# GpSimd's copies of the input into the second token order: from one block of sixteen to two blocks of eight, between and behind the rotations

## The chip, the cores and the metric

The kernel runs on one core of a Trainium2 chip. The metric is the device time of one execution in microseconds. The engines of the core are TensorE (PE; its weight loads are listed as PEld), VectorE (DVE), ScalarE (ACT), GpSimd (POOL) and SyncE (SP), which issues most DMAs. Each engine works through its own instructions in order and waits for others by semaphores.

## The reference

The reference is a decoder trunk of two layers on 512 tokens of 1024 channels, all in float32. Only the attention of the first layer matters here:

```python
qkv = xn @ w_qkv
q, k, v = jnp.split(qkv, 3, axis=-1)
q = apply_rope(q.reshape(B, T, A_HEADS, HEAD_DIM), cos, sin)
k = apply_rope(k.reshape(B, T, A_HEADS, HEAD_DIM), cos, sin)
...
for g, (window, r) in enumerate(A_GROUPS):
    ...
    o, lse = banded_attention(gather(q), gather(k), gather(v), window // r)
```

There are three groups of four heads, with (window, dilation) = (128, 1), (512, 4) and (2048, 16). With dilation r the tokens are taken in the order "every r-th token first": `gather` sorts the tokens by their place modulo r. The rotation (`apply_rope`) changes 16 of the 64 channels of every head of the queries and keys. Behind the attention come a gated convolutional feed-forward part, a second layer with full attention, and another feed-forward part.

## The kernel before, in words

Every large product is made of three float32r products: the operands are split into a high and a low part, and `mm3` (lines 228 to 231) adds high × high, high × low and low × high in PSUM. So the normed input of the first layer, transposed to channels × tokens, exists as four tiles: high and low part, each for channels 0 to 511 (index 0) and 512 to 1023 (index 1). They are called `xT` (line 549; xah and xal in the profile). Each is 128 partitions × 4 channel groups × 512 tokens.

Group 0 of the heads works on the tokens in their own order. Groups 1 and 2 work on a second order, in which the tokens are sorted by their place modulo 4. For these the kernel keeps the same four tiles once more with the tokens in that order, `xP` (line 550; xph and xpl). GpSimd makes them: `reorder(b)` (lines 556 to 562) copies the 128 tokens of block b, one instruction of 128 × 512 elements for each of the four tiles. Since each block of the second order has a quarter of its tokens from every block of the first, no part of `xP` can be used for a product before all four blocks are copied.

The order of the work in the first stage is written out by hand (lines 751 to 824), and each engine's instructions come in the order of these lines:

- Lines 751 to 781: for each token block, the norm, the transposes into `xT` (`transpose0`) and the query and key products of group 0 (`qk0`). `qk_post` (lines 569 to 582) follows for each block: ScalarE copies the product out of PSUM (line 573), then GpSimd rotates it with four instructions (lines 579 to 582). The four calls of `reorder` stand behind the rotations of blocks 0 and 1 and ahead of those of blocks 2 and 3.
- `v_proj0` (lines 708 to 724): the value products of group 0. Between them stand `qk_transpose(0, b)` (lines 584 to 591), in which TensorE transposes the rotated queries and keys and VectorE copies them out of PSUM (line 591), and `scores(0, 0)` and `scores(0, 1)`: TensorE's products of queries and keys (line 613), the softmax's first pass on VectorE (line 598) and the exponential on ScalarE (line 599).
- `wide_proj(1, ...)` (lines 783 to 797): the query and key products of group 1, on `xP`. It goes through the four weight tiles one by one, and for each through the four blocks. The first two weight tiles meet channels 0 to 511, the last two channels 512 to 1023. Between the weight tiles stand `p_transpose` (TensorE at line 635, ScalarE's copies at lines 637 and 640) and further scores of group 0.
- `wide_proj(2, ...)` and `wide_proj(1, "v_ps", ...)` follow for group 2 and for the values of both groups, and then the rest of the attention.

Weights come through the class `Weights` (lines 27 to 67): SyncE loads a tile, ScalarE writes its high part (line 49) and VectorE its low part (line 55), some tiles ahead of their use. The tiles of 8 KB per partition (weights, `xT`, `xP`, the queries and keys, the transposed probabilities) come from one pool of 17 buffers, so that new tiles take the place of old ones as soon as their last reader is done.

Of the kernel before, what the change touches and what calls it, by code (L numbers as in the profile page):

```python
# [8 lines left out]
F32 = mybir.dt.float32  # L9
# [7 lines left out]
NB = 4  # L17
# [53 lines left out]
def trunk_kernel(ctx, tc, x, norm_gains, w_qkv_a, w_o_a, w_q_b, w_o_b, kv_norm, w_kvf, b_f,  # L71
                 w_up, conv_w, conv_b, w_down, rope, out):
    nc = tc.nc
    act, dve, pool, pe, sp = nc.scalar, nc.vector, nc.gpsimd, nc.tensor, nc.sync
# [8 lines left out]
    def t8(shape, dt=F32, name="t8"):  # L83
        return p8.tile(shape, dt, tag="t8", name=name)
# [4 lines left out]
    def t2(shape, dt=F32, name="t2"):  # L89
        return p2.tile(shape, dt, tag="t2", name=name)  # L90

    def bank(shape, name="bank"):
        return psp.tile(shape, F32, tag="ps", name=name)
# [134 lines left out]
    def mm3(o, ah, al, bh, bl, first, last, shared=False):  # L228
        pe.matmul(o, ah, bh, start=first, stop=False, skip_group_check=shared)  # L229
        pe.matmul(o, ah, bl, start=False, stop=False, skip_group_check=shared)  # L230
        pe.matmul(o, al, bh, start=False, stop=last, skip_group_check=shared)  # L231
# [55 lines left out]
    def new_xT(name):  # L287
        hi = [t8([128, 4, T], F32R, name=f"{name}h{i}") for i in range(2)]
        lo = [t8([128, 4, T], F32R, name=f"{name}l{i}") for i in range(2)]
        return hi, lo  # L290
# [258 lines left out]
    xT = new_xT("xa")  # L549
    xP = new_xT("xp")  # L550
    xn = {}

    def by_fourth(a, spec="p k (l r) -> p k r l"):
        return a.rearrange(spec, r=4)

    def reorder(b):

        for part in range(2):
            for i in range(2):
                src = by_fourth(xT[part][i][:, :, b * 128:b * 128 + 128])  # L560
                dst = xP[part][i].rearrange("p k (r l) -> p k r l", r=4)[:, :, :, b * 32:b * 32 + 32]
                pool.tensor_copy(dst, src.bitcast(F32))

    def ax(g, b, kc):
        return xs(xP if g else xT, kc, slice(b * 128, b * 128 + 128))
# [3 lines left out]
    def qk_post(g, b, o):  # L569
        if b == 0:  # L570
            qks[g] = t8([128, 4, 8, HD], name=f"qk{g}")
        qk = qks[g][:, b]
        act.copy(qk.rearrange("p a d -> p (a d)"), o)
        tu = t2([128, 2, 8, 16], name="tu")
        rb = 4 * min(g, 1) + b
        c2 = rp[:, rb, None, 0:16].to_broadcast([128, 8, 16])
        s_lo = rp[:, rb, None, 16:24].to_broadcast([128, 8, 8])
        s_hi = rp[:, rb, None, 24:32].to_broadcast([128, 8, 8])
        pool.tensor_tensor(tu[:, 0], qk[:, :, 0:16], c2, ALU.mult)
        pool.tensor_tensor(tu[:, 1, :, 0:8], qk[:, :, 8:16], s_lo, ALU.mult)  # L580
        pool.tensor_tensor(tu[:, 1, :, 8:16], qk[:, :, 0:8], s_hi, ALU.mult)
        pool.tensor_tensor(qk[:, :, 0:16], tu[:, 0], tu[:, 1], ALU.add)
# [153 lines left out]
    def transpose0(b):  # L736
        transpose_in(b, xn.pop(b), xT)

    def qk0(b, *pieces):
        if b not in qk_banks:  # L740
            qk_banks[b] = bank([128, T], name="qk_ps")
        for s in pieces:
            if s not in ws:
                ws[s] = [t.rearrange("p (k c) -> p k c", k=2) for t in W.get()]
            wh, wl = ws[s]
            for k in range(2):
                kc = 2 * s + k
                ah, al = ax(0, b, kc)
                mm3(qk_banks[b], ah, al, wh[:, k, :], wl[:, k, :], kc == 0, kc == KD - 1)
# [18 lines left out]
    qk0(1, 3)  # L768
    qk_post(0, 0, qk_banks[0])
    qk_post(0, 1, qk_banks[1])  # L770
    qk0(2, 0, 1)
    transpose0(3)
    for b in range(NB):
        reorder(b)
    qk0(2, 2, 3)
    W.split(5)
    qk_post(0, 2, qk_banks[2])
# [1 line left out]
    W.ahead = 4  # L779
    W.split(6)  # L780
    qk_post(0, 3, qk_banks[3])

    def wide_proj(g, name, post, between):

        banks = [bank([128, T], name=name) for _ in range(4)]
        for s in range(4):
            w = W.get()
            wh, wl = (t.rearrange("p (k c) -> p k c", k=2) for t in w)
            for b in range(4):
                for k in range(2):  # L790
                    kc = 2 * s + k
                    ah, al = ax(g, b, kc)
                    mm3(banks[b], ah, al, wh[:, k, :], wl[:, k, :], kc == 0, kc == KD - 1)
                if s == 3:
                    post(g, b, banks[b])
            for f in between[s]:
                f()
# [348 lines left out]
    for n in range(N + 3):  # L1146
        live = n < N
        if live:
            j, i = units[n]
# [81 lines left out]
```

## Time and profile before

| | |
|---|---|
| median of 3 runs | 1174.08 us (1173.22 to 1174.54) |
| the profiled execution | 1175.93 us |
| its span in the profile | 1174.1 us |
| mean granted TensorE clock | 0.996 |
| GpSimd busy in 0 to 30, 30 to 60, 60 to 75 us | 7.21, 22.07, 0.00 us |
| VectorE busy in 30 to 60 us | 14.16 us |
| TensorE busy in 0 to 30, 30 to 60, 60 to 75 us | 27.64, 27.18, 14.84 us |

The profile is one execution, and its times count from the start of its span. A row of the timeline gives the start, the length, the engine, the line, the operation, the tiles it writes and reads, and how many instructions are merged in it; in brackets stands how long the engine was idle before it and what ended that. Matmuls overlap each other, so how long a row of them holds TensorE is read from the start of one row to the start of the next. The granted clock is the share of full speed that TensorE's clock was given.

### The profile page before, as it was taken

The page shows a single profiled execution, that of the slowest core. Times are in us where ns is not written, and L with a number is a line of the kernel's source. Part 1 is how long each engine was busy: PE and PEld are TensorE (multiplying, and loading weights), DVE is VectorE, ACT ScalarE, POOL GpSimd, SP SyncE. Part 2 cuts the span into 40 slices and gives each one's busy share as a digit, 9 for nine tenths or more (in the row PEclk, how much of TensorE's full clock was granted, in tenths as well). Part 3 has the DMA queues.
Part 4 walks back from the last instruction along what each step waited for, and adds up shares of the span by engine and source line. Part 5 has one row for each costly group of instructions (what it writes and reads, how often), then busy time and mean ns, then how long its engine had stood idle before and what let it go on. Part 6 is the DMA issues. An engine that isn't in the chain of part 4 may idle for free.

```text
span 1174.1 us, 15132 instructions
## 1 busy us (share of the span) xinstructions
PE 1157.1 (99%) x5898; PEld 962.0 (82%) x5898; DVE 666.9 (57%) x991; ACT 517.1 (44%) x900; POOL 204.2 (17%) x231
## 2 busy tenths in 40 slices
PE   9999999999999999999999999999999999999997
PEld 6788889888888888888778888789888888888886
DVE  6433477565566575406465688847565565575304
ACT  5354565433334354305462577755343333354202
POOL 2722000122122120000000466500122122120000
PEclk9899999999999999999999999999999999999999
DMA  8121064332333345302304343364333332344001
GB/s 292 54 91 55 1 166 126 90 105 79 103 108 88 92 137 189 88 1 58 107 1 127 90 118 117 91 201 126 90 92 88 108 105 78 105 132 173 1 1 71
DMA packets 134849, 115.72 MB, mean 99 GB/s; under 512 B 5753, under 2 KB 119913, under 8 KB 134778
## 3 DMA queue, kind: packets, MB, share of 16 engines
q1 hardware_dynamic: 133498, 110.57, 31.1%
q0 software_dynamic: 1280, 4.20, 1.5%
q8 instruction: 46, 0.75, 0.3%
q14 instruction: 25, 0.20, 0.1%
HBM read 108.41 MB, written 2.15 MB: 94 GB/s over the span
## 4 chain that ended last, share of the span: by engine, by line
PE 86%; DVE 5%; ACT 4%; POOL 2%; issue 2%; DVEq 0%; ACTq 0%
PE up L229 12%; PE up L230 12%; PE up L231 12%; PE acc L229 9%; PE acc L231 9%; PE acc L230 9%; PE v_ps L229 2%; PE v_ps L231 2%; PE v_ps L230 2%; PE qk_ps L229 1%; PE qk_ps L230 1%; PE qk_ps L231 1%; PE first L231 1%; PE first L229 1%; PE first L230 1%
## 5 line engine op out<-in xcount | busy, mean ns | idle before, releaser
L55 DVE TENSOR_TENSOR w<-wraw,w 128x1024 fp32r<-128x1024 f32 x182 | 264.6, 1480 | 94.3 <-ACT w L49 93.9
L49 ACT CAST w<-wraw 128x1024 fp32r<-128x1024 f32 x182 | 185.5, 1051 | 61.4 <-PE acc L231 38.2
L517 ACT ACTIVATE bb<-up,conv 128x512 f32<-128x512 f32 x80 | 62.6, 782 | 272.4 <-PE up L231 272.4
L525 POOL TENSOR_TENSOR hT<-bb 128x512 f32<-128x512 f32 x44 | 92.8, 2110 | 490.8 <-DVE bb L520 348.8
L518 DVE SCALAR_TENSOR_TENSOR bb<-up,conv,bb 128x511 f32<-128x511 f32 x80 | 60.0, 749 | 172.9 <-ACT bb L517 172.9
L229 PE MATMUL acc<-w,hs 128*128 128x512 f32 (+1 forms) x356 | 137.9, 387 | 1.1 <-DVE mix L276 1.1
L230 PE MATMUL acc<-w,hs 128*128 128x512 f32 (+1 forms) x356 | 137.6, 387 | 0.0
L231 PE MATMUL acc<-w,hs 128*128 128x512 f32 (+1 forms) x356 | 137.6, 387 | 0.0
L229 PE MATMUL up<-xbh,w 128*128 128x512 f32 x320 | 124.5, 389 | 0.0
L229 PE MATMUL up<-xch,w 128*128 128x512 f32 x320 | 124.5, 389 | 0.0
L230 PE MATMUL up<-xbl,w 128*128 128x512 f32 x320 | 124.5, 389 | 0.0
L230 PE MATMUL up<-xcl,w 128*128 128x512 f32 x320 | 124.5, 389 | 0.0
L231 PE MATMUL up<-xbh,w 128*128 128x512 f32 x320 | 124.5, 389 | 0.0
L231 PE MATMUL up<-xch,w 128*128 128x512 f32 x320 | 124.5, 389 | 0.0
L229 PEld LDWEIGHTS acc<-w,hs 128*128 128x128 f32 x356 | 66.8, 188 | 14.8 <-DVE mix L276 1.3
L230 PEld LDWEIGHTS acc<-w,hs 128*128 128x128 f32 x356 | 66.8, 188 | 13.7
L231 PEld LDWEIGHTS acc<-w,hs 128*128 128x128 f32 x356 | 66.8, 188 | 13.5
L231 PEld LDWEIGHTS up<-xbh,w 128*128 128x128 f32 x320 | 60.1, 188 | 12.6
L231 PEld LDWEIGHTS up<-xch,w 128*128 128x128 f32 x320 | 60.1, 188 | 12.6
L229 PEld LDWEIGHTS up<-xbh,w 128*128 128x128 f32 x320 | 60.1, 188 | 12.5
L230 PEld LDWEIGHTS up<-xcl,w 128*128 128x128 f32 x320 | 60.1, 188 | 12.5
L229 PEld LDWEIGHTS up<-xch,w 128*128 128x128 f32 x320 | 60.1, 188 | 12.3
(241 smaller groups left out, 2092.3 us busy)
## 6 DMA issues: line engine op xcount, KB each, us to landing
wraw<-in_w_up_dram SPq DMA_DIRECT2D x88, 512.0 KB
wraw<-in_w_down_dram SPq DMA_DIRECT2D x44, 512.0 KB
wraw<-in_w_kvf_dram SPq DMA_DIRECT2D x16, 512.0 KB
wraw<-in_w_qkv_a_dram SPq DMA_DIRECT2D x16, 256.0 KB
wraw<-in_w_q_b_dram SPq DMA_DIRECT2D x8, 512.0 KB
ck<-cd SPq DMA_DIRECT2D x8, 512.0 KB
qst<-qst POOLq DMA_DIRECT2D x16, 256.0 KB, 3.4
wraw<-in_w_o_b_dram SPq DMA_DIRECT2D x8, 512.0 KB
```

The lines of the kernel that those rows point to most:

```text
L49: self.nc.scalar.copy(pair[:, 0], raw)
L55: self.nc.vector.tensor_tensor(pair[:, 1], raw, pair[:, 0].bitcast(F32), ALU.subtract)
L229: pe.matmul(o, ah, bh, start=first, stop=False, skip_group_check=shared)
L230: pe.matmul(o, ah, bl, start=False, stop=False, skip_group_check=shared)
L231: pe.matmul(o, al, bh, start=False, stop=last, skip_group_check=shared)
L517: act.activation(bb[:, s, :], ps, AF.Identity, bias=cp[:, 3, ch:ch + 1], scale=cp[:, 2, ch:ch + 1])
L518: dve.scalar_tensor_tensor(bb[:, s, 1:], ps[:, :T - 1], cp[:, 1, ch:ch + 1], bb[:, s, 1:], ALU.mult, ALU.add)
L525: pool.tensor_tensor(hT[c // 4][:, c % 4, :], bb[:, 0, :], bb[:, 1, :], ALU.mult)
```

## The change

`reorder` takes several blocks, and within a call goes through the channel halves first, then the blocks, then the high and low part. It is called twice: for blocks 0 and 1 behind the rotations of blocks 0 and 1, and for blocks 2 and 3 behind the rotations of blocks 2 and 3. The number of copies, their shapes and their operands stay as they are.

```diff
-    def reorder(b):
-
-        for part in range(2):
-            for i in range(2):
-                src = by_fourth(xT[part][i][:, :, b * 128:b * 128 + 128])
-                dst = xP[part][i].rearrange("p k (r l) -> p k r l", r=4)[:, :, :, b * 32:b * 32 + 32]
-                pool.tensor_copy(dst, src.bitcast(F32))
+    def reorder(*blocks):
+
+        for i in range(2):
+            for b in blocks:
+                for part in range(2):
+                    src = by_fourth(xT[part][i][:, :, b * 128:b * 128 + 128])
+                    dst = xP[part][i].rearrange("p k (r l) -> p k r l", r=4)[:, :, :, b * 32:b * 32 + 32]
+                    pool.tensor_copy(dst, src.bitcast(F32))
...
     qk_post(0, 0, qk_banks[0])
     qk_post(0, 1, qk_banks[1])
+    reorder(0, 1)
     qk0(2, 0, 1)
     transpose0(3)
-    for b in range(NB):
-        reorder(b)
     qk0(2, 2, 3)
     W.split(5)
     qk_post(0, 2, qk_banks[2])
     qk0(3, 0, 1, 2, 3)
     W.ahead = 4
     W.split(6)
     qk_post(0, 3, qk_banks[3])
+    reorder(2, 3)
```

From line 557 on the changed kernel's lines stand one further down, so the copies are line 563 there, the rotations 580 to 583, the transposes 589 and the scores 614.

## The prediction

> **What bounds the kernel now.** I read the page first, then the waits of TensorE, then the first stage by windows, then its timeline.
>
> ```profile
> span 1174.1 us, 15132 instructions
> ## 1 busy us (share of the span) xinstructions
> PE 1157.1 (99%) x5898; PEld 962.0 (82%) x5898; DVE 666.9 (57%) x991; ACT 517.1 (44%) x900; POOL 204.2 (17%) x231
> ```
>
> TensorE is busy for 1157.1 of 1174.1 us, so a change off TensorE counts only where TensorE stands still or runs slow. GpSimd's own 204.2 us are worth nothing by themselves. The waits of TensorE over the whole span (total, times, longest) begin with the place that this change touches:
>
> ```profile
> PE qkT_ps L588 <- POOL qk L582: 2.8, 2, 2.4
> ```
>
> The longest is the transpose of the rotated queries and keys (L588), which waits for GpSimd's rotation (L582). The windows (length, busy time of PE, PEld, DVE, ACT, POOL, then clock, DMA share, GB/s) show that it costs more than those 2.8 us:
>
> ```profile
> 48.40:57.80 9.40, 6.58 (x29) 4.91 (x29) 3.72 (x18) 4.45 (x14) 3.67 (x9) 0.64 0.00 1
> 57.80:100.00 42.20, 42.04 (x221) 34.63 (x220) 14.06 (x43) 18.70 (x51) 7.23 (x16) 1.00 0.26 89
> 100.00:500.00 400.00, 399.84 (x2028) 336.19 (x2027) 235.60 (x296) 177.24 (x281) 55.24 (x40) 1.00 0.34 102
> ```
>
> ```profile
> 53.33:57.77 4.44, 4.44 (x20) 3.53 (x20) 3.00 (x16) 2.55 (x11) 0.00 (x0) 0.50 0.00 0
> 68.61:71.88 3.27, 3.11 (x25) 2.46 (x25) 2.00 (x11) 1.53 (x7) 0.00 (x0) 1.00 0.00 0
> ```
>
> From 53.33 to 57.77 the granted clock is 0.50. A mean of 0.64 over the 9.4 us comes out when it is 0.50 for 9.4 × 0.36 / 0.5 = 6.8 us of them, the last ones: from about 51.0 to 57.8. The stall is followed by 6.8 us at half speed. Its timeline there (start, length):
>
> ```profile
> 48.02 0.28 PE L230 MATMUL v_ps<-w,xah 128*128 128x256 f32 x1
> 48.14 0.28 PE L231 MATMUL v_ps<-w,xal 128*128 128x256 f32 x1
> 50.79 1.05 PE L588 MATMUL qkT_ps<-ident,qk 128*128 128x128 f32 x4 [2.37 <-POOL qk L582]
> 52.28 1.11 PE L588 MATMUL qkT_ps<-ident,qk 128*128 128x128 f32 x4 [0.45 <-POOL qk L582]
> 53.33 3.09 PE L613 MATMUL s_ps<-qkT 64*128 64x128 f32 x16
> 56.35 0.79 PE L229 MATMUL qk_ps<-w,xph 128*128 128x512 f32 x1
> ...
> 57.77 0.39 PE L229 MATMUL qk_ps<-w,xph 128*128 128x512 f32 x1
> ```
>
> Between the last value product (48.14) and the fourth product of the second projection (57.77) stand eight transposes, sixteen score rows and three products. And here is why GpSimd is late:
>
> ```profile
> 27.17 2.19 POOL L562 CAST xph<-xah 128x512 fp32r<-128x512 f32 x2
> ...
> 37.57 3.24 POOL L562 CAST xph<-xah 128x512 fp32r<-128x512 f32 x2
> ...
> 49.19 0.45 POOL L579 TENSOR_TENSOR tu<-qk,rope 128x128 f32<-128x128 f32 x1
> ...
> 51.78 0.45 POOL L582 TENSOR_TENSOR qk<-tu 128x128 f32<-128x128 f32 x1
> ```
>
> Sixteen copies (L562) run without a pause from 27.17 to 49.19. The rotations of token blocks 2 and 3 stand behind them and end at 52.23.
>
> **The change, part by part.** No instruction is added or taken away on any engine; GpSimd's are put in another order. In the instruction order of the changed kernel, eight copies (blocks 0 and 1) follow the rotations of blocks 0 and 1, then come the eight rotation instructions of blocks 2 and 3, then the other eight copies: four of channels 0 to 511 first, then four of the rest. No DMA moves. TensorE gains waits: the first products of wide_proj(1) wait for GpSimd's low copies, those of its third weight for the high ones. In GpSimd's queue the late copies move behind the rotations; behind them stand the rotations of group 1, whose input comes only from products that need the copies anyway.
>
> *Rotations, the part on the path.* The first eight copies now take 27.17 to 37.57 (the eight of before have the same shapes, and ScalarE and VectorE write blocks 0 and 1 earlier still). The rotations take 52.23 − 49.19 = 3.04, so they end at 40.6. Their input of block 3 is there:
>
> ```profile
> 36.09 0.59 ACT L573 COPY qk<-qk_ps 128x512 f32<-128x512 f32 x1 [3.90 <-PE qk_ps L231]
> ```
>
> It ends at 36.7. TensorE asks for the rotations at 48.26, 7.6 us after their end. Both waits at L588, 2.8 us, go.
>
> *What is late next* is the copies in front of wide_proj(1). Copies have two lengths, and so have VectorE's weight splits (L55) beside them (shortest, median, longest, in ns):
>
> ```profile
> L562 POOL CAST xph<-xah x8: 1092/1134/2153, 27.2 to 46.0; 128x512 fp32r<-128x512 f32 x8
> ```
>
> ```profile
> L55 DVE TENSOR_TENSOR w<-wraw,w x4: 1224/2150/2157, 37.7 to 59.9; 128x1024 fp32r<-128x1024 f32 x4
> ```
>
> ```profile
> 37.66 6.30 DVE L55 TENSOR_TENSOR w<-wraw,w 128x1024 fp32r<-128x1024 f32 x3 [4.12 <-ACT w L49]
> 43.89 0.68 DVE L591 COPY qkT<-qkT_ps 128x512 f32<-128x512 f32 x1
> ```
>
> At the short length sixteen copies would take 16 × 1.09 = 17.4; they took 22.0, so some 4.6 us are lost to splits, about 1.05 a split. Three splits (37.66 to 43.96) now meet the rotations and the first late copies. No row shows a rotation beside a split. Its price is between nothing and one whole short split each, 3 × 1.22 = 3.7; I take the copies' 1.05, the nearest row; even at 3.7 the rotations end at 44.3, in time. The low copies then end at 37.57 + 3.04 + 4 × 1.09 + 3 × 1.05 = 48.1 (45.0 without any loss; 52.9 with 3.7 on the rotations and all four copies at 2.15). TensorE wants them at 50.9 (below): 2.8 us of cover, and at the bad end 2.0 us of a new wait. The high copies end at 52.5, at 56.7 if all four are long, at 61.5 from the bad end. They are wanted 15.5 us behind the first wide product (56.35 to 71.88, next fence), at 66.4.
>
> *VectorE beside the late copies.* The copies of 48 to 52 us lie beside VectorE's L591 and its softmax, as none did before. L591 took 0.68 at 43.89 with a copy beside it: no price. The softmax has no such row; I take nothing, and at most the splits' factor, 2.15 / 1.22, on its first 2 us or so: 1.5 us. What hides it: the transposes that need it stand a full weight's products (6.2 us) behind the scores, and scores and exponentials took 3.2 us (53.33 to 56.49):
>
> ```profile
> 56.10 0.39 ACT L599 ACTIVATE p<-p,st 128x128 f32<-128x128 f32 x1
> ```
>
> ```profile
> 62.59 0.60 PE L635 MATMUL pT_ps<-ident,p 128*128 128x128 f32 x4
> ```
>
> ScalarE's L640 and three weight casts (L49) wait for late copies because they reuse the copied tiles' memory; the queue behind them waits too. The earliest, L640, comes after those transposes, 57 us in the new count, later than every copy it needs.
>
> *The sum.* What the stretch takes at full clock, from the same work elsewhere:
>
> ```profile
> 41.64 1.04 PE L588 MATMUL qkT_ps<-ident,qk 128*128 128x128 f32 x8
> 42.44 0.36 PE L229 MATMUL v_ps<-w,xah 128*128 128x256 f32 x1
> ```
>
> ```profile
> 68.61 2.10 PE L613 MATMUL s_ps<-qkT 64*128 64x256 f32 x16
> 70.81 1.31 PE L635 MATMUL pT_ps<-ident,p 128*128 128x128 f32 x8
> 71.88 0.48 PE L229 MATMUL qk_ps<-w,xph 128*128 128x512 f32 x1
> ```
>
> ```profile
> 96.98 1.56 PE L615 MATMUL s_ps<-qkT 64*128 64x128 f32 x16
> 98.47 0.50 PE L229 MATMUL qk_ps<-w,xph 128*128 128x512 f32 x1
> ...
> 99.27 0.40 PE L229 MATMUL qk_ps<-w,xph 128*128 128x512 f32 x1
> ```
>
> Eight transposes: 42.44 − 41.64 = 0.80. Scores: half are 128 wide, half 256; 1.49 for sixteen of one kind, 2.20 of the other, so 1.85 (between 1.51, half of what they took at half clock, and 2.20). Three products: 0.80. The last value product holds TensorE until 48.14 + 0.12 = 48.26. So the first wide product starts at 48.26 + 0.80 + 1.85 = 50.9 and the fourth at 51.7, where it started at 57.77: **6.1 us less**, 5.7 to 6.4 by the bounds of the scores. Of this 2.8 is the stall and 3.3 the half clock. Behind 57.8 TensorE stands busy (42.04 of 42.20 us, then 399.84 of 400) and everything that feeds it is released by its own progress; the DMA share in the stretch is 0.00, so no transfer is being waited out. The gain goes to the end.
>
> The profiled execution took 1175.93 (span 1174.1 and 1.8 around it), 1.85 above the median of 1174.08. 1175.93 − 6.1 = 1169.8 against it, or **1168.0** against the median.
>
> **The rivals.**
>
> *The stall goes, the low clock stays.* If transposes and short scores are too light to keep the clock, the new stretch (2.65 us of them) still halves it for some 6.8 us and loses 3.4: the gain is 2.7, **1171.4**. Against it stands the window 68.61 to 71.88: 3.27 us of scores and transposes at 1.00. For it: the clock fell after only 2.4 us without work. The Trainium skill, "TensorE: Matmul & The Clock Gate", Part 1, has the clock fall after an idle window of about 3.4 us and rise after a busy one. By that rule 2.4 us alone would not do it, the light work around the stall would have to count as idle, and the sum would be this rival's. The trace disagrees on the length but agrees that a fall is paid for over more than one window.
>
> *The wait moves to wide_proj(1), and the kernel is slower.* Place: the first wide product, which waits for the four late low copies. If every copy, early and late, takes the long 2.15, they end at 27.17 + 12 × 2.15 + 3.04 = 56.0. TensorE idles 5.1 us, the clock halves, and 6.8 us at half follow: 56.0 + 0.80 + 3.4 = 60.2 against 57.77, 2.4 us slower, **1176.5**. It breaks even where the copies end at 53.6. For it: copies do double beside splits. Against: only about five of sixteen did, and VectorE has no splits between 43.96 and the softmax. The Trainium skill, "SBUF — State Buffer", "Who interferes with whom", lets a VectorE instruction with two SBUF inputs contend with GpSimd's reads and one with at most one input there not. By it the softmax (one input in PSUM) would lengthen no copy; the 0.68 of L591 agrees for a PSUM copy, and no run here shows it for the softmax.
>
> *Nothing is gained*, because rotations stay late or a later wait takes it back: **1174.1**. The instruction order and the 7.6 us of cover speak against the first, the busy windows against the second.
>
> **How the numbers follow.** The forecast gets 0.82, the low clock 0.06, the moved wait 0.06 (0.04 of it slower), nothing gained 0.06. Faster by over 0.2% (2.35 us, about what a measurement can tell from no change): 0.82 + 0.06 + 0.01 = 0.89. Within: 0.06 + 0.01 = 0.07; slower: 0.04. The forecast's own range is 1167.7 to 1168.4 by the sum, and the three runs of before lie 0.9 below to 0.5 above their median, so 1166.8 to 1168.9. At the bad end of the low copies, a wait of 2.0, the time is 1170.0; I take 1166.8 to 1170.2, which leaves out the three rivals, 0.18.
>
> **What would show it.** Right: no wait at L588, transposes at about 48.3, the first wide product near 50.9, rotations ended by 41 to 44, clock 1.00 throughout 48 to 58, TensorE 1.00 busy there. Wrong: a wait of the first wide product for L563 (the copies' line after), a clock of 0.50 anywhere up to 60, a split or softmax longer than 2.2, or a TensorE wait behind 60 us that is new.

## The result, and the profile after

The changed kernel takes 1169.16 us (median of 6 runs, 1168.86 to 1169.52); the kernel before, run beside it, takes 1173.76 (6 runs, 1172.74 to 1175.50). The ratio is 0.996, with a 95% interval of 0.9947 to 0.9972: faster by 4.6 us, 0.4%. The prediction said 1168.0, with a range of 1166.8 to 1170.2. The profiled execution took 1168.88, with a span of 1167.1, 7.0 us shorter than that of before.

The waits of TensorE over the whole span of the changed kernel no longer have a row of GpSimd; those of the second layer lead:

```profile
PE o_ps L1120 <- ACT pT L1107: 1.5, 1, 1.5
PE v_ps L229 <- ACT xkh L431: 1.4, 1, 1.4
```

The window of the stall (columns as in the prediction: length, busy time of five engines, granted clock, DMA share, GB/s) and the one behind it:

```profile
48.40:57.80 9.40, 9.40 (x57) 7.70 (x56) 4.74 (x19) 7.46 (x24) 3.57 (x4) 1.00 0.00 1
57.80:100.00 42.20, 42.14 (x224) 34.80 (x223) 14.68 (x42) 19.07 (x50) 7.21 (x16) 1.00 0.30 100
```

TensorE is busy for all of the 9.40 us, where it was for 6.58, and the clock is 1.00, where it was 0.64. Its timeline in that place:

```profile
48.05 0.28 PE L231 MATMUL v_ps<-w,xal 128*128 128x256 f32 x1
48.17 1.04 PE L589 MATMUL qkT_ps<-ident,qk 128*128 128x128 f32 x8
49.13 1.68 PE L614 MATMUL s_ps<-qkT 64*128 64x128 f32 x16
50.75 0.50 PE L229 MATMUL qk_ps<-w,xph 128*128 128x512 f32 x1
...
51.55 0.39 PE L229 MATMUL qk_ps<-w,xph 128*128 128x512 f32 x1
```

The eight transposes follow the value products at once, and the fourth wide product starts at 51.55 instead of 57.77: 6.2 us earlier. GpSimd's timeline shows why:

```profile
36.43 1.13 POOL L563 CAST xpl<-xal 128x512 fp32r<-128x512 f32 x1
37.52 0.46 POOL L580 TENSOR_TENSOR tu<-qk,rope 128x128 f32<-128x128 f32 x1
37.95 1.30 POOL L581 TENSOR_TENSOR tu<-qk,rope 128x64 f32<-128x64 f32 x1
39.21 1.31 POOL L582 TENSOR_TENSOR tu<-qk,rope 128x64 f32<-128x64 f32 x1
40.59 1.32 POOL L583 TENSOR_TENSOR qk<-tu 128x128 f32<-128x128 f32 x1
...
42.97 0.46 POOL L583 TENSOR_TENSOR qk<-tu 128x128 f32<-128x128 f32 x1
43.38 1.13 POOL L563 CAST xph<-xah 128x512 fp32r<-128x512 f32 x1
...
46.59 1.14 POOL L563 CAST xpl<-xal 128x512 fp32r<-128x512 f32 x1
...
50.85 1.11 POOL L563 CAST xpl<-xal 128x512 fp32r<-128x512 f32 x1
```

The rotations end at 43.4, 4.7 us before TensorE asks for them; the low copies (channels 0 to 511) end at 47.7, 3.0 us before the first wide product; the high ones (channels 512 to 1023) at 52.0. Three of the rotation's instructions last 1.3 us; they met VectorE's weight splits.

So the mechanism is the one forecast: the rotations come early, the wait goes, and the clock stays up. What didn't fit was the size: between the two profiles the stretch gained 6.2 and the spans 7.0, and the medians only 4.6.

### The profile page after: what moved, and what is told of

Its sections match the earlier page's. It is cut to its first block, busy times and chain, and to the rows that moved or that the text cites. A ratio compares the mean times of both kernels' runs of the same rounds, so it can differ in the third digit from the quotient of the medians.

```text
span 1167.1 us, 15131 instructions
## 1 busy us (share of the span) xinstructions
PE 1153.6 (99%) x5898; PEld 960.1 (82%) x5898; DVE 663.8 (57%) x991; ACT 515.8 (44%) x900; POOL 203.9 (17%) x231
## 4 chain that ended last, share of the span: by engine, by line
PE 89%; DVE 5%; ACT 3%; issue 2%; DVEq 0%; ACTq 0%
PE up L231 12%; PE up L229 12%; PE up L230 12%; PE acc L229 9%; PE acc L230 9%; PE acc L231 9%; PE v_ps L229 2%; PE v_ps L231 2%; PE v_ps L230 2%; PE qk_ps L230 2%; PE qk_ps L229 2%; PE qk_ps L231 2%; PE first L229 1%; PE first L230 1%; PE first L231 1%
## 5 line engine op out<-in xcount | busy, mean ns | idle before, releaser
L517 ACT ACTIVATE bb<-up,conv 128x512 f32<-128x512 f32 x80 | 62.4, 780 | 272.8 <-PE up L231 272.8
L231 PEld LDWEIGHTS up<-xch,w 128*128 128x128 f32 x320 | 60.1, 188 | 12.6
L230 PEld LDWEIGHTS up<-xbl,w 128*128 128x128 f32 x320 | 60.1, 188 | 12.5
```

The source lines that it names most:

```text
L517: act.activation(bb[:, s, :], ps, AF.Identity, bias=cp[:, 3, ch:ch + 1], scale=cp[:, 2, ch:ch + 1])
```

## The experiments

**Theory A**: the half clock behind the stall has no fixed length; the profiled execution of before had a long one, and in the median less of it was saved. **Theory B**, the rival: the half clock is always the same, and 1.5 us of the gain are given back later. Further rivals were about which half of the change does it. The time of the kernel before, run beside the experiments, had a median of 1175.74 in the first four and of 1174.64 in the last four.

**The kernel before again** (no edit).

> The kernel before, unchanged, run again to see how its executions differ from each other. The change gained 4.6 us in the medians (1173.76 to 1169.16), 6.2 in the stretch between the two profiles and 7.0 over their spans. Theory A: the half clock behind the stall isn't of one length; it was 6.8 us in the profiled execution and is shorter in most. Then the executions of this kernel spread by some 3 us, from about 1172.5 to 1176, the fast ones with a mean granted clock near 1.000 and the slow ones near 0.996, and a new profile shows the half clock at another place or length, with the same wait of about 2.4 us at the transposes. Theory B: the half clock is the same in every execution and some 1.5 us of the gain are given back later. Then clock and time hardly vary (0.996, within 1 us) and the profile looks as it did.

Measured: 1175.16 (11 runs, 1172.95 to 1175.92), ratio 0.9996 (0.9987 to 1.0005). With all runs of the unchanged kernel whose clock was listed there are 55 executions, with a median of 1175.01. By their mean granted clock:

| clock | executions | shortest, median, longest (us) |
|---|---|---|
| 0.999 | 8 | 1172.74, 1173.03, 1173.91 |
| 0.998 | 12 | 1174.27, 1174.81, 1175.19 |
| 0.997 | 5 | 1173.91, 1174.14, 1175.02 |
| 0.994 to 0.996 | 30 | 1174.56, 1175.77, 1176.69 |

They spread over 4.0 us, and the short ones have nearly the full clock. The classes overlap because the clock also falls at other places: in the last microseconds, in which TensorE has nothing left to do (0.50 and 0.00 us busy in the last 2 us of the new profile), and in some executions in the second layer (below). Time and clock vary as theory A has it, and not as B has it. The new profile, by windows:

```profile
48.40:57.80 9.40, 6.67 (x31) 4.92 (x30) 3.33 (x15) 4.07 (x13) 4.06 (x10) 0.64 0.00 1
```

Here the fall was as long as in the first profile (mean 0.64), in an execution of 1175.50. This profile by itself would have fitted B too.

**The stall filled.** Products that nothing reads keep TensorE at work while it waits:

```diff
+    def fill(n):
+        o = bank([128, 512], name="fill")
+        for _ in range(n):
+            pe.matmul(o, xT[0][0][:, 0, 0:128], xT[0][0][:, 0, :], start=True, stop=True)
...
-             [L(qk_transpose, 0, 2), L(qk_transpose, 0, 3), ...
+             [L(fill, 10), L(qk_transpose, 0, 2), L(fill, 4), L(qk_transpose, 0, 3), ...
```

> The kernel before, with products that nothing reads put into the stall: ten 128x512 products ahead of the transposes of block 2 and four ahead of those of block 3. TensorE is kept at work while it waits, so the stall stays and the half clock should go. At full clock the waits alone cost what lies between 48.26 (or 48.2) and the end of the last rotation, 52.2, less one block's transposes, 0.4: 3.6 us. Theory A (the clock's share differs from execution to execution, 1 us on average): 1169.2 + 3.7 = 1172.9, with a spread of under 1 us, so 0.9 below the kernel before. Theory B (the clock always costs 2.5 us beyond the wait): the same 3.7 above the changed kernel if nothing is given back, but 2.5 below the kernel before: 1171.3. Rival: the clock has nothing to do with idleness; then the profile still shows 0.50 behind 51 us and the time is that of before, 1173.8.

Measured: 1173.04 (11 runs, 1172.69 to 1173.63), ratio to before 0.9983 (0.9974 to 0.9992). The window and the timeline of TensorE:

```profile
48.40:57.80 9.40, 9.34 (x53) 7.10 (x52) 3.73 (x18) 5.68 (x19) 3.71 (x9) 1.00 0.00 1
```

```profile
48.31 2.46 PE L809 MATMUL fill<-xah 128*128 128x512 f32 x10
50.82 0.66 PE L588 MATMUL qkT_ps<-ident,qk 128*128 128x128 f32 x4
51.23 1.17 PE L809 MATMUL fill<-xah 128*128 128x512 f32 x4
52.33 0.66 PE L588 MATMUL qkT_ps<-ident,qk 128*128 128x128 f32 x4
...
55.32 0.39 PE L229 MATMUL qk_ps<-w,xph 128*128 128x512 f32 x1
```

Useless work made the kernel faster: the transposes are as late as before (50.82 and 52.33), but the clock stays at 1.00 and the fourth wide product comes at 55.32. The spread shrinks to 0.9 us. What is left above the changed kernel, 1173.04 − 1169.16 = 3.9, is the price of the wait alone, against 3.7 expected. The rest of what the kernel before loses is mostly the clock's, and it varies. Against the kernel before run beside it the gain is 2.7 and not the 0.9 expected, because that kernel's median came out at 1175.74 here and not at 1173.76; by theory B the time would have been 1171.3.

**The first half of the change alone**: two calls, but the old order of the channels in a call.

```diff
-        for i in range(2):
-            for b in blocks:
-                for part in range(2):
+        for b in blocks:
+            for part in range(2):
+                for i in range(2):
```

> The change's first half alone: two calls, between and behind the rotations, but with the order of before inside a call (block, part, channel half). GpSimd ended all copies at 52.0 in the changed kernel, and TensorE wanted the low ones of the last block at 50.8 (high part) and 51.3 (low part). In this order the last low copies end at about 49.8 (high part) and 50.9 (low part). Theory: the place of the copies is the whole gain and the order of the channels is worth nothing here: 1169.2, within 0.5 of the changed kernel, with no wait of TensorE. Rival: the order is needed, a wait of up to 1 us at the first wide products appears: 1170 or more.

Measured: 1169.25 (5 runs, 1169.14 to 1170.08), ratio to before 0.9954 (0.9940 to 0.9968). No wait of TensorE for GpSimd. The order of the channels is worth nothing where the copies stand in two parts.

**All copies behind the rotations, low channels first**: the first call taken out, the second made for all four blocks.

```diff
-    reorder(0, 1)
...
-    reorder(2, 3)
+    reorder(0, 1, 2, 3)
```

> All sixteen copies behind the rotations of blocks 2 and 3, low channels first. The rotations of block 3 wait for ScalarE's copy until 36.7 and end at 38 to 39; eight low copies at 1.07 and some 3 us lost to the three weight splits end at about 50, wanted at 50.8; the high ones end at about 58.5, wanted at 65. Theory: the cover still holds, with under 1 us to spare: 1169.2, at most 1170 if the low copies are a little late. Rival (the copies must be in two parts for the gain): a wait of 2 us or more at the first wide product, and time between 1171 and that of before, 1173.8.

Measured: 1169.22 (5 runs, 1168.91 to 1169.49), ratio to before 0.9951 (0.9939 to 0.9964). GpSimd's first copy, the last of the eight low ones (channels 0 to 511) and the first high one:

```profile
38.90 2.13 POOL L563 CAST xph<-xah 128x512 fp32r<-128x512 f32 x1
...
48.43 1.11 POOL L563 CAST xpl<-xal 128x512 fp32r<-128x512 f32 x1
49.49 1.11 POOL L563 CAST xph<-xah 128x512 fp32r<-128x512 f32 x1
```

The low copies end at 49.5 (50 expected), and the first wide product starts at 50.6: the cover holds with 1 us to spare, and there is no wait. The two parts aren't needed either, if the low channels come first.

**All copies behind, in the old order**: both edits above together.

> All sixteen copies behind the rotations, as in the run before, but in the old order (block, part, channel half): the rival of the prediction in which the wait moves to the wide products. The copies end at about 58.5; the last low high-part copy ends at about 55.0 and the last low low-part copy at about 57.1, wanted at 50.8 and 51.3. TensorE's first wide product waits 4.2 us, its third another 1.7, and the fourth starts at about 57.4, 5.9 behind the changed kernel. Theory A (the clock falls behind a wait of this length in most executions, at up to 3.4 us): 1175.1 without, 1178.5 with the whole fall; the median between, 1176 to 1178, so slower than the kernel before by up to 0.2%. Rival (the wait costs only itself): 1175.1. Rival (the order hardly matters, as in the two-part kernel): 1169.2.

Measured: 1177.09 (11 runs, 1176.08 to 1178.59), ratio to before 1.0024 (1.0015 to 1.0032): slower. TensorE's timeline:

```profile
49.30 1.68 PE L614 MATMUL s_ps<-qkT 64*128 64x128 f32 x16
55.16 0.50 PE L229 MATMUL qk_ps<-w,xph 128*128 128x512 f32 x1 [4.18 <-POOL xph L563]
55.49 0.58 PE L230 MATMUL qk_ps<-w,xph 128*128 128x512 f32 x1
57.21 0.80 PE L231 MATMUL qk_ps<-w,xpl 128*128 128x512 f32 x1 [1.14 <-POOL xpl L563]
57.80 0.63 PE L229 MATMUL qk_ps<-w,xph 128*128 128x512 f32 x1
```

The wait has moved to the wide products: 4.18 for the high parts (xph) and 1.14 for the low parts (xpl) of channels 0 to 511, and the products behind it last 0.63 instead of 0.39, at half clock (0.50). This is the prediction's rival that loses, as a kernel: with everything late, the order of the channels decides 7.9 us (1169.22 against 1177.09).

**The second half of the change alone**: all sixteen copies in their old place, low channels first.

> All sixteen copies where the kernel before has them, ahead of the rotations of blocks 2 and 3, but low channels first: the change's second half alone. The rotations still end at 52.2, so the transposes wait as before. Theory: nothing is gained, the time is that of the kernel before, 1173 to 1176 with its spread. Rival: the order of the channels gains by itself: 1172 or less.

Measured: 1175.12 (11 runs, 1173.05 to 1176.07), ratio 1.0002 (0.9993 to 1.0011): nothing gained. Its profile caught an execution of 1173.05, with the stall and without the fall of the clock:

```profile
48.40:57.80 9.40, 6.23 (x40) 4.78 (x39) 3.73 (x18) 5.63 (x19) 3.76 (x9) 1.00 0.00 1
```

```profile
50.88 0.66 PE L589 MATMUL qkT_ps<-ident,qk 128*128 128x128 f32 x4 [2.34 <-POOL qk L583]
52.37 0.66 PE L589 MATMUL qkT_ps<-ident,qk 128*128 128x128 f32 x4 [0.84 <-POOL qk L583]
```

The wait for block 2 is the 2.3 to 2.4 us of every profile, but the clock is 1.00 and the second wait is 0.84 instead of 0.45, since the transposes between the two waits go at full speed.

**Two more profiles of the kernel before.**

> The kernel before once more, for another profile. Theory A: the wait at the transposes is 2.4 us again and the half clock is again 6.8 us long or shorter, by whole or partial windows of the clock; the time of this execution follows it: 1172.7 to 1173 without a fall, 1174 to 1174.5 with half of it, 1175.5 to 1176 with all. If time and clock in the stretch don't go together, theory A falls.

> The same as the run before: one more profile of the kernel before. Theory A: the fourth wide product starts between 55.4 (no fall of the clock) and 58.2 (a fall of 6.8 us), and the execution's time minus that start is the same within 1 us in all profiles of this kernel.

Measured: 1176.69 and 1174.94. The first has the clock at half for 6.8 us again, from 51.7 to 58.5. The second, by windows:

```profile
53.00:53.50 0.50, 0.50 (x10) 0.50 (x9) 0.50 (x1) 0.00 (x0) 0.00 (x0) 0.81 0.00 0
53.50:56.50 3.00, 3.00 (x13) 2.16 (x11) 2.11 (x16) 2.27 (x11) 0.00 (x0) 0.50 0.00 0
56.50:57.00 0.50, 0.50 (x3) 0.40 (x2) 0.37 (x4) 0.50 (x3) 0.00 (x0) 0.78 0.00 0
```

At 0.50 for 0.19 + 3.00 + 0.22 = 3.4 us, half as long, and begun 2.4 us later than in the first profile (53.3 against 50.9). Side by side, with the stretch from the start of the last value product to that of the fourth wide product (57.77 − 48.14 in the first profile):

| profile | half clock in this place | stretch | execution |
|---|---|---|---|
| before, first profile | 6.8 us | 9.6 us | 1175.93 |
| before again | 6.8 us | 9.4 us | 1175.50 |
| before, third profile | 6.8 us | 9.6 us | 1176.69 |
| before, fourth profile | 3.4 us | 8.7 us | 1174.94 |
| old place, low first | none | 7.1 us | 1173.05 |
| stall filled | none | 7.1 us | 1173.35 |
| the change | none | 3.5 us | 1168.88 |

Execution and stretch go together: their difference lies between 1165.4 and 1167.1 in all seven.

The two parts in the old order and all copies behind, low channels first, have 1165.8 and 1165.5, with a stretch of 3.5. All behind in the old order has 1168.3, with a stretch of 9.6: there the half clock lasts from 55.5 to 62.4 and so goes on for 4.6 us behind the stretch. Two expectations were missed by little: the third and fourth executions lie 0.7 and 0.4 us above the times expected for their falls, and time less start of the fourth wide product differs by 1.25 us among the four profiles of before, not by under 1. Most of that comes from the second layer (next section). For the stretch, theory A holds: the same wait costs 3.6 us (7.1 − 3.5) without a fall of the clock and up to 6.1 with the long one.

## Why the prediction was right, and where it was off

*The bound and the place* were right: the longest wait of TensorE went, and nothing behind it took its place.

*The rotations* were forecast to end at 40.6, or 44.3 with a whole split on each of three; they ended at 43.4. Next to a split an instruction of 0.32 took 1.30, so 0.98 each: the 1.05 borrowed from the copies was close, only it fell on the rotations and not on the low copies. "No row shows a rotation beside a split" was wrong: the profile of before has one in group 1, where the first rotation instruction took 1.02 instead of 0.46 beside a split that ended at 81.35:

```profile
80.12 1.23 DVE L55 TENSOR_TENSOR w<-wraw,w 128x1024 fp32r<-128x1024 f32 x1 [2.54 <-ACT w L49]
80.65 1.02 POOL L579 TENSOR_TENSOR tu<-qk,rope 128x128 f32<-128x128 f32 x1 [28.42 <-DMA wraw<-in_w_qkv_a_dram]
```

In the changed kernel the low copies ended at 47.7 (48.1 forecast), the high ones at 52.0 (52.5).

*The softmax beside the copies*: no price, as taken. In the changed kernel its instructions of 128 columns follow each other at 0.21, as they did without a copy beside them, and the copies beside it took their short length, 1.11 and 1.12:

```profile
50.01 0.28 DVE L599 CUSTOM_DVE_ANT_0 p<-s_ps,mask 128x128 f32<-128x128 f32 x1
50.22 0.08 DVE L599 DVE_READ_ACCUMULATOR2_ANT st<- 128x1 f32 x1
50.22 0.28 DVE L599 CUSTOM_DVE_ANT_0 p<-s_ps,mask 128x128 f32<-128x128 f32 x1
```

*The stretch at full clock*: 3.45 forecast for transposes, scores and three products; 51.55 − 48.17 = 3.38 measured. In part two misses offset each other: the transposes took 0.96 (0.80 taken) and the scores 1.62 (1.85 taken). The first wide product came at 50.75 (50.9 forecast), the fourth at 51.55 (51.7).

*The sum against the median* is the step that failed. The prediction took "6.1 us less" from the profiled execution and then took the same 6.1 from the median, 1174.08. But the profiled execution was 1.85 above that median, and it had a cost in it that is in the sum and that other executions lack in part or whole: its clock had fallen for 6.8 us, and the table above has executions of the same kernel with 3.4 us and a time of 1174.94. Against its own execution the forecast was 1169.8, and the change's runs have a median of 1169.16. How long the clock fell in the three runs themselves is not on record. The median of the 55 later executions, 1175.01, lies in the middle: 0.92 below the profiled execution and 0.93 above the median of the three runs, so the small sample had as large a share in the miss as the profile. What could have told it beforehand were the two numbers that the prediction put side by side: an execution that is 1.85 above a median whose runs lie within 0.9 of it may pay for something that they don't.

*The range* held in part by luck. By the sum and the spread of before it was 1166.8 to 1168.9, and 1169.16 lies above that. The upper end of 1170.2 was there for a new wait of 2.0 us at the first wide product, and no such wait came.

*The split of the gain*, "2.8 is the stall and 3.3 the half clock", was off too. Without any fall of the clock the wait costs 3.6, because the transposes of block 2, when they go at full speed, only wait longer for block 3. So the clock's share in these profiles is 0 to 2.5 and not 3.3. The change gains 3.6 to 6.1 in the stretch, from one execution to the next; from the median of the 55 executions of before, 1175.01, to that of the changed kernel it is 5.85.

*Given back or gained elsewhere*: the spans differ by 7.0, the stretch by 6.1. Another 0.1 lies ahead of it. At the first query product of the second layer the distance is 6.4 (632.4 to 626.0), behind its attention it is 7.0 (745.5 to 738.5). TensorE's waits for ScalarE's transposed probabilities there were 2.0 us in the first profile of before and 1.5 in the changed kernel; with the copies in the old place they are 1.5 in four later profiles and 2.0 in one (the third of before), so this isn't the change's doing. At the same place, from about 741 to 749 us, the clock was at 0.50 for 3.4 us in four of the ten profiles: the third and fourth of before, the stall filled, and all behind in the old order. From the first query product of the second layer to the end of the span it is 541.1 to 541.3 us with neither, 541.7 with the longer wait, 541.7 to 541.8 with the fall, and 542.1 with both. So up to 1 us of the differences between executions comes from the second layer, wherever the copies stand.

*The rivals.* "The stall goes, the low clock stays" didn't happen: the clock stayed at 1.00 through 2.6 us of transposes and short scores. "The wait moves" was wrong for this order of the copies and near in its price: break-even at 53.6, 1176.5 for copies that end at 56.0; the kernel with all copies behind in the old order had its wide products at 55.2 and 57.2, and took 1177.09. "Nothing is gained" fell with the result.

## What to carry to other kernels

Before taking a term of one profile from a median of runs, ask whether that execution was a typical one for just this term, and whether a median of three runs is settled. A wait of TensorE that makes the clock fall has a fixed part and a part that differs from execution to execution, and a change that removes it narrows the spread as well. In a queue that serves two consumers, order the work by when each result is wanted. Here the short, urgent rotations had to go ahead of the late copies, and one of two more things was needed with it: halving the copies, or sorting their channels. With either the whole gain came, with neither the kernel was slower than before, and sorting without moving gained nothing. Work that nothing reads can show what a clock costs apart from the wait itself.

## What the runs showed of the hardware

The fall of the clock came in steps: none, 3.4 or 6.8 us at half, at the same two waits of 2.3 to 2.4 us and of 0.4 to 0.8, and it began anywhere from 50.8 to 53.3 us. The Trainium skill, "TensorE: Matmul & The Clock Gate", Part 1, gives a window of 3.4 us that runs freely, without regard to the kernel; the two lengths agree with one and two of them, and the differing start with the free running. So a fall was paid for over one window or two, and not always over more than one, as the prediction has it. The Trainium skill, in the same part of that page, has the clock fall after at least one idle window; that does not agree as it stands. In two profiles of the kernel before (falls at 50.9 and 50.8) the first wait of 2.3 to 2.4 us alone came before the fall, and in the second layer the clock fell in four of ten profiles behind a wait of 1.5 us. In the kernel with all copies behind in the old order the clock was still 1.00 through a wait of 4.18 us, until 55.5, and then at half for 6.8 us.

GpSimd and VectorE also share the loss in a way that had not been expected. Three splits beside long copies took 6.30 us in the kernel before; beside the rotations they took 4.03:

```profile
37.57 4.03 DVE L55 TENSOR_TENSOR w<-wraw,w 128x1024 fp32r<-128x1024 f32 x3 [4.11 <-ACT w L49]
```

GpSimd lost about as much in both cases (1.0 us a split). So VectorE's splits lost less here beside short instructions than beside long ones, while GpSimd lost the same. The length of GpSimd's instruction isn't all of it, though: one split of the changed kernel took only 1.34 with a long copy beside it (split from 32.12, copy of 2.07 from 32.33). What decides was not tested.
